# A hybrid two-layer trunk: x loaded first, one norm for all tokens, and the first projections with the features as the outer loop

## The chip, the cores and the metric

The kernel runs on one core of a Trainium2 chip. The metric is the device time of one execution in microseconds (us), as the median of repeated runs. TensorE (PE in the rows) does the matrix products, VectorE (DVE), ScalarE (ACT) and GpSimd (POOL) the elementwise work, and transfers are issued from the queues of SyncE (SP) and ScalarE.

## The reference, cut to what matters

A step of a flow-matching model: 128 context tokens and 512 latent tokens, 1024 features, two layers. The even layer has attention (grouped queries) and a gated DeltaNet behind one combined input projection, the odd layer a Mamba-2 scan, and each layer a squared-ReLU MLP. Shift, scale and gate of every sub-layer come from SiLU(cond) by a weight matrix `w_mod`. What the change touches is the beginning of the even layer:

```python
mod = (jax.nn.silu(cond) @ w_mod[layer] + b_mod[layer])[:, None, :]
sh1, sc1, g1, sh2, sc2, g2 = jnp.split(mod, 6, axis=-1)
h = rms_norm(x, norm_mix_g) * (1 + sc1) + sh1
aq, ak, av, dqkv, dz, dbeta, dalpha = _split(h @ w_in, EVEN_SPLITS)
# attention from aq, ak, av; delta rule from dqkv, gated by dz, with
beta = sigmoid(dbeta)
log_decay = -exp(a_log) * softplus(dalpha + dt_bias)
```

`aq` has 512 columns; `ak`, `av`, `dbeta` and `dalpha` together have 272. All is float32.

## The kernel before, in words

A float32 operand is held as two halves of the format fp32r, `hi` and `lo`, and a product is three matrix products: hi·hi, hi·lo, lo·hi. A weight block is loaded as 1 MB into a tile `wraw` on SyncE's queue (`wload`, L264), cast to `whi` on ScalarE (L272), and `wlo` is the rest (L275). When `self.share` is set, L275 alternates between VectorE and GpSimd by the count `self.turn`. The normed and modulated activations stand as `hh` and `hl`, features on partitions, eight groups k of 128 features.

A list scheduler orders each engine's instructions: the program is written in one order, and a simulated timeline decides what is issued first on each engine. An engine then runs its own list strictly in that order; a waiting instruction holds up all behind it.

The start, in `even()`: xt, 2.5 MB, is loaded on ScalarE's queue (L728), beside the first `w_mod` blocks on SyncE's. `token_r` works out the norm's factor twice, for tokens 0 to 319 and 320 to 639: squares on ScalarE (L577), sums over features on TensorE (L579, L585), an inverse root on VectorE (L234 to L239), and a broadcast on TensorE (L594) with a copy (L596) as `rb`. `mod_first` makes shift and scale in four chunks c of two feature groups each, from two 1 MB blocks a chunk (L516, product `modps`). `modulate` makes `hh` and `hl` (L622 to L624), for all eight groups of the first half of the tokens, then of the second. The combined projection (L750, product `atps`) has three column blocks as its outer loop: first the 272 columns, then twice 256 of the queries; inside it the five groups of 128 tokens, and innermost k and the three products. Each group's sum has one PSUM bank and is copied to `qkv` (L752).

`gates` (L883 to L915) makes beta and the log decay from 16 of the 272 columns (`gxa`, softplus in L246 to L257, `gg`), sums the decays over the chunk on TensorE (L904, from `gg`), and transposes them there (L911, from `gc`).

What follows is called the delta stage here: `delta_in` for four heads (L300, products `gps` of 322 columns with the convolutions on VectorE, L658 to L680, of which `vt` feeds `kvps`, L870), the preparation of attention between head 0 and head 1 (`att_prep`; rms factors in L1159 to L1161, scaling in L1194 and L1195, rotation in L1203 to L1208, four pieces of it on GpSimd in L1206), and the next chunks of the modulation (`mod_steps`, loads in L466, products in L459). It ends where `X` is fetched back from `growd` (L933).

Of the kernel before, what the change touches and what calls it, by code (L numbers as in the profile page):

```python
# [11 lines left out]
F32 = mybir.dt.float32  # L12
F32R = mybir.dt.float32r
I32 = mybir.dt.int32
AF = mybir.ActivationFunctionType
ALU = mybir.AluOpType
# [24 lines left out]
AS, HB = 10, 4  # L41
# [161 lines left out]
class Prog:  # L203
# [293 lines left out]
    def mod_first(self, pools, gates):  # L497

        nc = self.nc
        n = 0  # L500
        for c in range(4):
            raws = []
            if c == 1:
                gates()
            for kh in range(2):
                raw = pools[n % len(pools)].tile([P, 2048], F32, name="wraw", tag="wraw")
                n += 1
                o = self.widx["mod0", c, kh]
                self.behind = nc.sync.dma_start(out=raw, in_=self.io["wall"][o:o + P * 2048].rearrange("(p x) -> p x", p=P))
                raws.append(raw.rearrange("p (k m c) -> p k m c", k=4, c=P))  # L510
            if c == 3:
                self.setup_rest()
            ps = self.pmod.tile([P, 512], F32, name="modps", tag="mod")
            for k in range(KT):
                for r in range(4):
                    nc.tensor.matmul(ps[32 * r:32 * r + 32, :P], self.condst[:, k, 32:64], raws[k // 4][:, k % 4, :, 32 * r:32 * r + 32],  # L516
                                     start=k == 0, stop=k == KT - 1)
            t = self.small.tile([P, P], F32, name="modt", tag="modt")
            nc.vector.transpose(out=t, in_=ps[:, :P])
            cut = lambda ap: ap.rearrange("p (q m) o -> p q m o", q=2)[:, :, 2 * c:2 * c + 2]  # L520
            b = self.par(("bmod", 0))[:, 0:16].rearrange("p (m o) -> p m o", o=1)
            nc.vector.tensor_tensor(out=cut(self.mod[0][:, 0:16, :]), in0=t.rearrange("p (q m c) -> p q m c", q=2, c=32)[:, :, :, 0:3:2],
                                    in1=cut(b).to_broadcast([P, 2, 2, 2]), op=ALU.add)
# [44 lines left out]
    def token_r(self, pool, tiles, n, hf):  # L568

        nc = self.nc  # L570
        nk = len(tiles)
        c = slice(hf * HU, (hf + 1) * HU)
        inv = 1.0 / n
        ps = self.pn.tile([P, 512], F32, name="stps", tag="n")
        for k, x in enumerate(tiles):
            sq = pool.tile([P, HU], F32, name="sq", tag="sq", bufs=4)
            nc.scalar.activation(out=sq, in_=x[:, c], func=AF.Square)  # L577
            r = 32 * (k % 4)
            nc.tensor.matmul(ps[r:r + 32, :HU], self.ones32, sq, start=k < 4, stop=k >= nk - 4)  # L579
        st = pool.tile([P, HU], F32, name="st", tag="st")  # L580
        nc.vector.tensor_copy(st, ps[:, :HU])
        cuts = ((0, 128), (128, 256), (256, 320))
        pc = self.pn.tile([P, 512], F32, name="stc", tag="n")
        for t, (a, b) in enumerate(cuts):
            nc.tensor.matmul(pc[:b - a, t:t + 1], st[:, a:b], self.cst("stat"), start=True, stop=True)  # L585
        ms = pool.tile([P, 3], F32, name="ms", tag="ms", bufs=2)
        r = pool.tile([P, 3], F32, name="rr", tag="rr", bufs=2)
        nc.vector.memset(ms[64:, 2:3], 1.0)
        nc.vector.tensor_scalar(out=ms[:, 0:2], in0=pc[:, 0:2], scalar1=inv, scalar2=EPS, op0=ALU.mult, op1=ALU.add)
        nc.vector.tensor_scalar(out=ms[:64, 2:3], in0=pc[:64, 2:3], scalar1=inv, scalar2=EPS, op0=ALU.mult, op1=ALU.add)  # L590
        self.rsqrt(pool, r, ms, [P, 3])
        pb = self.pn.tile([P, 512], F32, name="rbps", tag="n")
        for t, (a, b) in enumerate(cuts):
            nc.tensor.matmul(pb[:, a:b], r[:b - a, t:t + 1].to_broadcast([b - a, P]), self.ident[:b - a, :b - a], start=True, stop=True)  # L594
        rb = pool.tile([P, HU], F32, name="rb", tag=f"rb{hf}")
        nc.vector.tensor_copy(rb, pb[:, :HU])  # L596
        return rb

    def modulate(self, h, pool, rbs):


        nc = self.nc
        a = pool.tile([P, KT, 2], F32, name="mA", tag="mA")
        n = KT // 4
        for c in range(0, KT, n):
            nc.vector.scalar_tensor_tensor(out=a[:, c:c + n], in0=self.modv(0, 1)[:, c:c + n], scalar=1.0,
                                           in1=self.par(("gmix", 0))[:, c:c + n].rearrange("p (m o) -> p m o", o=1).to_broadcast([P, n, 2]),
                                           op0=ALU.add, op1=ALU.mult)
        sh = self.modv(0, 0)
        hh, hl = h  # L610

        plan = (((slice(1, 129), CTX_U, 0), (slice(130, 322), slice(128, HU), 1)), ((slice(322, 642), slice(HU, NTOK), 1),))
        self.padding(pool, h)

        def half(hf):
# [1185 lines left out]
```

## Time and profile before

| | us |
|---|---|
| median of 3 runs | 2151.09 (2150.94 to 2152.92) |
| profiled execution, device time | 2148.23 |
| profiled execution, span of the trace | 2146.4 |
| TensorE busy in the span | 2054.9 (96%) |
| VectorE, ScalarE, GpSimd busy | 1373.3, 898.4, 153.4 |
| start: until the last product of the combined projection | 0 to 87.4 |
| delta stage | 88.2 to 225.1 |

The device time of the profiled execution is 1.8 us more than its span and 2.9 us less than the median of the runs. In rows of the timeline the first two columns are start and duration in us. Matrix products overlap on TensorE, so the time that one costs in a stream is the step between two starts, not its duration.

### The profile page before, as it was taken

How to read it: one execution, taken by the hardware profiler on the slowest of the kernel's cores; microseconds unless marked ns; L12 is line 12 of the kernel's file. 1: busy time of each engine (PE TensorE's matmuls, PEld its weight loads, DVE VectorE, ACT ScalarE, POOL GpSimd, SP SyncE). 2: the span in 40 equal slices, each digit the busy share in tenths (PEclk: the TensorE clock that was granted, in tenths of full speed). 3: DMA queues.
4: the chain of work that ended last, by engine and by line, in shares of the span. 5: the costliest groups of instructions: out<-in, count | busy, mean ns of one | idle time of the engine just before them, and what ended most of it. 6: DMA issues, size and time to landing. Idle time of an engine off the chain costs nothing.

```text
span 2146.4 us, 32954 instructions
## 1 busy us (share of the span) xinstructions
PE 2054.9 (96%) x13339; PEld 1846.3 (86%) x13339; DVE 1373.3 (64%) x2585; ACT 898.4 (42%) x1892; POOL 153.4 (7%) x112
## 2 busy tenths in 40 slices
PE   6999799899899999999899999999999899999998
PEld 4999787787797989898799999999888898989896
DVE  6376776865787767673678886787644734344445
ACT  4345444444342323233258876666531322323131
POOL 1041301300000000000000001111110000000000
PEclk9999799899999999999999999999999999999999
DMA  8261100005255344332224433343341221212121
GB/s 328 91 234 40 39 1 18 18 1 201 80 194 193 138 140 155 138 119 103 89 83 162 132 135 120 120 138 123 107 168 69 89 97 61 79 59 99 59 79 50
DMA packets 56106, 233.32 MB, mean 109 GB/s; under 512 B 6602, under 2 KB 21458, under 8 KB 34194
## 3 DMA queue, kind: packets, MB, share of 16 engines
q1 hardware_dynamic: 45952, 216.63, 28.6%
q10 hardware_dynamic: 10002, 14.58, 1.9%
q8 instruction: 105, 1.72, 0.3%
q14 instruction: 47, 0.39, 0.1%
HBM read 222.76 MB, written 8.43 MB: 108 GB/s over the span
## 4 chain that ended last, share of the span: by engine, by line
PE 89%; DVE 7%; DMA 3%; ACT 1%; issue 1%; DVEq 0%; SPq 0%; ACTq 0%
PE gps L300 41%; PE rps L328 28%; PE atps L750 2%; PE yps L1704 2%; PE avps L1331 2%; DMA wraw<-wall 1%; PE offps L1718 1%; PE dps L1038 1%; PE stps L1735 1%; PE scps L1273 1%; DMA X<-growd 1%; PE dps L1032 1%; PE xkps L1554 1%; PE modps L459 1%; PE scps L1303 1%
## 5 line engine op out<-in xcount | busy, mean ns | idle before, releaser
L300 PE MATMUL gps<-hh,whi 128*128 128x322 f32 (+3 forms) x1552 | 488.4, 316 | 1.4 <-ACT hh L412 1.4
L300 PE MATMUL gps<-hh,wlo 128*128 128x322 f32 (+3 forms) x1552 | 486.4, 314 | 0.0
L300 PE MATMUL gps<-hl,whi 128*128 128x322 f32 (+3 forms) x1552 | 485.3, 313 | 0.0
L300 PEld LDWEIGHTS gps<-hh,whi 128*128 128x128 f32 (+1 forms) x1552 | 292.3, 189 | 7.9 <-issue 4.4
L300 PEld LDWEIGHTS gps<-hl,whi 128*128 128x128 f32 (+1 forms) x1552 | 292.4, 188 | 3.2 <-issue 2.8
L300 PEld LDWEIGHTS gps<-hh,wlo 128*128 128x128 f32 (+1 forms) x1552 | 292.4, 188 | 2.1 <-issue 1.6
L328 PE MATMUL rps<-wlo,hidh 128*128 128x512 f32 x640 | 253.3, 396 | 0.0
L328 PE MATMUL rps<-whi,hidh 128*128 128x512 f32 x640 | 252.3, 396 | 0.0
L328 PE MATMUL rps<-whi,hidl 128*128 128x512 f32 x640 | 250.5, 395 | 0.0
L272 ACT CAST whi<-wraw 128x1024 fp32r<-128x1024 f32 (+2 forms) x132 | 140.0, 1062 | 252.3 <-PE rps L328 176.3
L284 DVE TENSOR_TENSOR wlo<-wraw,whi 128x1024 fp32r<-128x1024 f32 x88 | 107.5, 1224 | 187.4 <-ACT whi L283 187.3
L300 PE MATMUL gps<-yh,whi 128*128 128x320 f32 x1024 | 227.1, 311 | 0.2 <-ACT yh L412 0.2
L275 DVE TENSOR_TENSOR wlo<-wraw,whi 128x1024 fp32r<-128x1024 f32 (+3 forms) x123 | 157.9, 1285 | 101.6 <-ACT whi L272 101.1
L283 ACT CAST whi<-wraw 128x1024 fp32r<-128x1024 f32 x88 | 91.8, 1048 | 266.2 <-PE rps L328 183.3
L300 PEld LDWEIGHTS gps<-yh,whi 128*128 128x128 f32 x1024 | 172.5, 189 | 1.0 <-ACT yh L412 0.7
L300 PE MATMUL gps<-yh,wlo 128*128 128x320 f32 x512 | 158.6, 310 | 0.0
L328 PEld LDWEIGHTS rps<-whi,hidh 128*128 128x128 f32 x640 | 120.3, 188 | 29.4 <-issue 1.2
L328 PEld LDWEIGHTS rps<-wlo,hidh 128*128 128x128 f32 x640 | 120.3, 188 | 28.8 <-issue 0.6
L328 PEld LDWEIGHTS rps<-whi,hidl 128*128 128x128 f32 x640 | 120.3, 188 | 28.6
L485 DVE SCALAR_TENSOR_TENSOR macc<-wraw,condst,macc 128x512 f32<-128x512 f32 x196 | 136.6, 746 | 6.0 <-ACT macc L488 5.9
L650 DVE TENSOR_SCALAR hr<-gps 128x320 f32<-128x320 f32 x128 | 62.6, 489 | 105.8 <-PE gps L300 105.5
L651 ACT ACTIVATE hr<-hr 128x320 f32<-128x320 f32 x128 | 60.1, 470 | 151.8 <-DVE hr L650 150.3
(428 smaller groups left out, 3560.9 us busy)
## 6 DMA issues: line engine op xcount, KB each, us to landing
wraw<-wall SPq DMA_DIRECT2D x158, 1024.0 KB
bc<-afs SPq DMA_DIRECT2D x40, 512.0 KB
Q<-afr SPq DMA_DIRECT2D x64, 128.0 KB
xt<-xt ACTq DMA_DIRECT2D x1, 2560.0 KB
X<-growd SPq DMA_DIRECT2D x8, 320.0 KB
x<-x ACTq DMA_DIRECT2D x1, 2560.0 KB
xd<-x ACTq DMA_DIRECT2D x1, 2560.0 KB
x<-xd SPq DMA_DIRECT2D x1, 2560.0 KB
```

What stands on the lines that cost most here:

```text
L272: self.nc.scalar.copy(out=hi, in_=raw[:, :, c:c + m])
L275: eng.tensor_tensor(out=lo, in0=raw[:, :, c:c + m], in1=hi.bitcast(F32), op=ALU.subtract)
L283: self.nc.scalar.copy(out=hi, in_=x)
L284: self.nc.vector.tensor_tensor(out=lo, in0=x, in1=hi.bitcast(F32), op=ALU.subtract)
L300: self.nc.tensor.matmul(ps, ws[k // KT][q // 2][:, k % KT, :], xs[q % 2][k][:, c], start=k == 0 and q == 0, stop=k == n - 1 and q == 2)
L328: nc.tensor.matmul(ps, parts[x][k][:, c], w[y][:, j, :], start=k == 0 and q == 0, stop=k == n - 1 and q == 2)
L485: nc.vector.scalar_tensor_tensor(out=a, in0=x, scalar=w, in1=a, op0=ALU.mult, op1=ALU.add)
L650: nc.vector.tensor_scalar(out=r, in0=ps, scalar1=0.0, scalar2=None, op0=ALU.max)
L651: nc.scalar.activation(out=r, in_=r, func=AF.Square)
L750: nc.tensor.matmul(ps[:, :n], x[k][:, TOFF[t]:TOFF[t] + P], w[:, k, :], start=k == 0 and q == 0, stop=k == KT - 1 and q == 2)
L1331: nc.tensor.matmul(acc, val(c, i), p, start=c == 1, stop=c == 6)
L1704: nc.tensor.matmul(py[q * 64:q * 64 + 64, pr * P:(pr + 1) * P], X[t](1 + d)[:, hh * 64:hh * 64 + 64], D[t][:, d, hh, :], start=d == 0, sto ...
```

## The change

Order of loading: xt comes first, in two halves on SyncE's queue; then the blocks of chunk 0 of `w_mod`, the two query blocks of the projection, the other chunks, and only then the constants and the block of 272 columns.

The norm is made once for all 640 tokens (`token_rows` for `token_r`). The loop over the chunks c holds everything: `mod_first(c)`, then `modulate(c)` for two feature groups and all tokens, then these two groups' products with all 512 query columns, in five PSUM banks that stay open over the four chunks. The 272 columns come after that, token group by token group, and then `gates`. `self.turn` and `self.share` are set behind the projection, so that the alternation of L275 between VectorE and GpSimd starts with another parity.

```diff
-                xload = nc.scalar.dma_start(out=self.xt, in_=io["xt"])
+                for a in (0, KT // 2):
+                    self.behind = nc.sync.dma_start(out=self.xt[:, a:a + KT // 2], in_=io["xt"][:, a:a + KT // 2])
...
-                rbs = [self.token_r(xp, [self.xt[:, k, :] for k in range(KT)], D, hf) for hf in range(2)]
-                blocks = ((272, 0), (256, 272), (256, 528))
-                watt = []
-                self.turn = 1
-                self.mod_first([self.raw, raw0], lambda: watt.append(self.wpart(self.wload(("att", 0), 272, wa), 0, 272, wa)))
+                raws = [self.landed(land, ("mod0", 0, kh)) for kh in range(2)]
+                rb = self.token_rows(xp)
...
-                half = self.modulate(h, xp, rbs)
-                self.share = True
-                half(0)
-                half(1)
-                for b, (n, c0) in enumerate(blocks):
-                    hi, lo = watt[0] if b == 0 else self.wpart(self.wload(("att", b), n, wa), 0, n, wa)
-                    for t in range(NT):
-                        ps = self.pg.tile([P, 512], F32, name="atps", tag="g")
-                        for k in range(KT):
-                            for q, (x, w) in enumerate(((xs[0], hi), (xs[0], lo), (xs[1], hi))):
-                                nc.tensor.matmul(ps[:, :n], x[k][:, TOFF[t]:TOFF[t] + P], w[:, k, :],
...
+                for c in range(4):
+                    self.mod_first(c, raws)
+                    if c == 0:
+                        for j in range(2):
+                            x = self.landed(land, ("att", 1 + j)).rearrange("p (k c) -> p k c", c=256)
...
+                    if c < 3:
+                        raws = [self.landed(land, ("mod0", c + 1, kh)) for kh in range(2)]
+                    else:
+                        self.setup_rest()
+                    self.modulate(c, h, xp, rb)
+                    for k in (2 * c, 2 * c + 1):
+                        for t in range(NT):
+                            for q, (x, w) in enumerate(triples(wq)):
+                                nc.tensor.matmul(acc[t], x[k][:, TOFF[t]:TOFF[t] + P], w[:, k, :], start=k == 0 and q == 0, stop=k == KT - 1 and q == 2)
+                wk = self.wpart(self.wload(("att", 0), 272, wa), 0, 272, wa)
+                for t in range(NT):
+                    nc.scalar.copy(out=qkv[:, t, 272:784], in_=acc[t])
+                for t in range(NT):
+                    ps = self.pg.tile([P, 512], F32, name="atps", tag="g")[:, :272]
+                    for k in range(KT):
+                        for q, (x, w) in enumerate(triples(wk)):
+                            nc.tensor.matmul(ps, x[k][:, TOFF[t]:TOFF[t] + P], w[:, k, :], start=k == 0 and q == 0, stop=k == KT - 1 and q == 2)
+                    nc.scalar.copy(out=qkv[:, t, 0:272], in_=ps)
+                self.turn, self.share = 1, True
                 self.behind = None
                 self.gates(xp, self.pmod, qkv, gt)
```

Three places of the order. On TensorE, the end of the combined projection before (`atps` of the last query columns, then the sums of the gates from `gg`, then the delta stage):

```order
L750 MATMUL atps<-wlo,hh 128x256
L750 MATMUL atps<-whi,hl 128x256
L904 MATMUL gps<-gg,con 128x20 [waits DMAHW5_49,DVE_49,PE_49]
L904 MATMUL gps<-gg,con 128x20 x3
L300 MATMUL gps<-hh,whi 128x322
L300 MATMUL gps<-hl,whi 128x322
```

The same place now, where the last `atps` is of the 272 columns:

```order
L749 MATMUL atps<-wlo,hh 128x272
L749 MATMUL atps<-whi,hl 128x272
L903 MATMUL gps<-gg,con 128x20 [waits DMAHW7_49,DVE_49,PE_49]
L903 MATMUL gps<-gg,con 128x20 x3
L910 MATMUL gps<-con,gc 40x128 [waits DVE_49,Activation_49]
L300 MATMUL gps<-hh,whi 128x322
```

The sums of the gates now stand behind the very columns that they are made from, and the transpose of `gc` (L910, L911 before) has come ahead of the first L300. On VectorE, the gates before, behind the last `hl` of the modulation:

```order
L624 SCALAR_TENSOR_TENSOR hl<-htmp,mod_71,hh 128x320 [waits Activation_49] x2
L894 TENSOR_TENSOR gxa<-qkv,prm 128x40 [waits Activation_49]
L246 SCALAR_TENSOR_TENSOR spe<-gxa 128x40 [waits DVE_49]
L275 TENSOR_TENSOR wlo<-wraw,whi 128x2048 [waits DMAHW7_49,PE_49,Activation_49]
L892 TENSOR_SCALAR beta<-gx 128x20 [waits Activation_49]
```

And now, where `kst` and `asel` are small preparations of attention:

```order
L609 SCALAR_TENSOR_TENSOR hl<-htmp,mod_71,hh 128x512 [waits Activation_49]
L1215 CAST kst_1386<-ones_72 64x1792 [waits PE_49]
L1217 TENSOR_TENSOR asel<-con 4x2 [waits DMAHW3_49]
L893 TENSOR_TENSOR gxa<-qkv,prm 128x40 [waits Activation_49]
L891 TENSOR_SCALAR beta<-gx 128x20 [waits Activation_49]
```

The cast of `kst`, which stood behind the gates before, now stands ahead of them and itself waits for TensorE. On GpSimd, the begin of the delta stage before:

```order
L1168 MEMSET vc 128x640 [waits PE_49,Pool_49]
L275 TENSOR_TENSOR wlo<-wraw,whi 128x1024 [waits PE_49,DMAHW1_49,Activation_49,Pool_49]
L275 TENSOR_TENSOR wlo<-wraw,whi 128x1024 [waits DMAHW3_49,PE_49,Activation_49]
L1206 TENSOR_TENSOR ar<-qkv,con 128x10x16 [waits DMAHW5_49,DVE_49]
L1206 TENSOR_TENSOR ar<-qkv,con 128x10x16 x3
```

And now:

```order
L1167 MEMSET vc 128x640 [waits DVE_49,PE_49]
L1205 TENSOR_TENSOR ar<-qkv,con 128x10x16 [waits DMAHW2_49,DMAHW7_49,DVE_49,Activation_49]
L1205 TENSOR_TENSOR ar<-qkv,con 128x10x16 x3
L275 TENSOR_TENSOR wlo<-wraw,whi 128x1024 [waits PE_49,DMAHW2_49,Activation_49,Pool_49]
L1205 TENSOR_TENSOR ar<-qkv,con 128x10x16 [waits DVE_49]
```

The low half of head 0's second weight block (L275) now stands on GpSimd behind the first four pieces of the rotation, where two such pieces stood ahead of all rotations.

## Rows read from the trace of the kernel before

**Rows 1.** The page: its chain of waits by engine

```profile
PE 89%; DVE 7%; DMA 3%; ACT 1%; issue 1%; DVEq 0%; SPq 0%; ACTq 0%
```

**Rows 2.** Windows: us, busy by engine, clock, DMA share, GB/s

```profile
0.00:14.00 14.00, 1.94 (x32) 1.39 (x32) 1.47 (x11) 1.50 (x2) 0.20 (x4) 1.00 0.86 349
14.00:25.00 11.00, 7.67 (x118) 4.71 (x118) 4.68 (x14) 6.44 (x13) 0.00 (x0) 1.00 1.01 419
88.20:225.10 136.90, 135.68 (x1220) 130.66 (x1220) 96.33 (x195) 65.29 (x181) 35.59 (x28) 1.00 0.34 119
```

**Rows 3.** TensorE's waits: engine, line, releaser, total us, times, longest

```profile
PE atps L750 <- DVE hl L624: 3.6, 1, 3.6
...
PE kvps L870 <- DVE vt L679: 0.7, 1, 0.7
```

**Rows 4.** Timeline of ScalarE: squares behind xt, cast of a query block

```profile
14.94 1.55 ACT L577 ACTIVATE sq<-xt 128x320 f32<-128x320 f32 x4 [8.37 <-DMA xt<-xt]
...
40.05 1.89 ACT L272 CAST whi<-wraw 128x2048 fp32r<-128x2048 f32 x1
```

**Rows 5.** Timeline of VectorE: the modulation at 41, the low half at 62

```profile
41.17 6.21 DVE L622 SCALAR_TENSOR_TENSOR htmp<-xt,mA,rb 128x320 f32<-128x320 f32 x4
...
61.99 2.29 DVE L275 TENSOR_TENSOR wlo<-wraw,whi 128x2048 fp32r<-128x2048 f32 x1 [1.37 <-ACT whi L272]
```

**Rows 6.** Timeline of GpSimd: the start and the first rotations

```profile
42.02 4.54 POOL L275 TENSOR_TENSOR wlo<-wraw,whi 128x2048 fp32r<-128x2048 f32 x1 [41.58 <-ACT whi L272]
...
113.09 2.61 POOL L275 TENSOR_TENSOR wlo<-wraw,whi 128x1024 fp32r<-128x1024 f32 x1 [15.47 <-ACT whi L272]
117.93 4.06 POOL L1206 TENSOR_TENSOR ar<-qkv,con 128x160 f32<-128x160 f32 x4 [2.24 <-DVE qkv L1195]
```

**Rows 7.** Chain of waits: start us, us, what

```profile
60.65 1.32 PE gps L300 x9
61.98 25.38 PE atps L750 x216
```

**Rows 8.** Timeline of TensorE: one chunk's half; 512 columns; the gates' sums

```profile
21.39 1.08 PE L516 MATMUL modps<-wraw,condst 128*32 128x128 f32 x32
...
87.20 0.96 PE L904 MATMUL gps<-gg,con 128*128 128x20 f32 x8
...
654.81 0.40 PE L328 MATMUL rps<-whi,hidh 128*128 128x512 f32 x1
...
657.14 0.40 PE L328 MATMUL rps<-wlo,hidh 128*128 128x512 f32 x1
```

**Rows 9.** Window behind the wait that ended at 47.9

```profile
48.00:52.00 4.00, 4.00 (x20) 0.57 0.00 0
```

**Rows 10.** Timeline of VectorE: the gates, and attention's first cast

```profile
60.18 0.20 DVE L894 TENSOR_TENSOR gxa<-qkv,prm 128x40 f32<-128x40 f32 x1 [3.91 <-ACT qkv L752]
...
64.20 0.25 DVE L892 TENSOR_SCALAR beta<-gx 128x20 f32<-128x20 f32 x2
64.36 0.18 DVE L248 TENSOR_SCALAR spz<-spe 128x40 f32<-128x40 f32 x1
...
67.80 0.20 DVE L899 SCALAR_TENSOR_TENSOR gg<-gg,gea 128x40 f32<-128x40 f32 x1
...
87.34 1.09 DVE L1216 CAST kst<-ones 64x1792 fp32r<-64x1792 f32 x1 [19.35 <-PE atps L750]
```

**Rows 11.** The delta stage: VectorE's scaling (timeline), then the chain

```profile
110.42 5.97 DVE L1194 TENSOR_TENSOR qkv<-qkv,ars 128x640 f32<-128x640 f32 x5
...
127.39 1.07 DVE vt L679
...
225.07 6.63 DMA X<-growd
```

More of the change, by code (lines that the diff above doesn't have):

```diff
@@ L495, in mod_steps @@
             yield
-    def mod_first(self, pools, gates):
-        nc = self.nc
[L500 to L513, printed above, removed]
-            for k in range(KT):
[L515 to L523, printed above, removed]
@@ L565, in setup_rest, with token_rows @@
         nc.vector.tensor_scalar(out=self.prm[:, a:b], in0=self.prm[:, a:b], scalar1=0.5, scalar2=None, op0=ALU.mult)
-    def token_r(self, pool, tiles, n, hf):
+    def token_rows(self, pool):
         nc = self.nc
[L571 to L582, printed above, removed]
-        pc = self.pn.tile([P, 512], F32, name="stc", tag="n")
[L584 to L596, printed above, removed]
-        return rb
@@ L599, in modulate @@
[L599 to L608, printed above, removed]
+        pl, pc = (self.pn.tile([P, 512], F32, name="stps", tag="n") for _ in range(2))
@@ new lines, in token_rows @@
+        for k in range(KT):
+            sq = pool.tile([P, NTOK], F32, name="sq", tag="sq", bufs=2)
+            nc.scalar.activation(out=sq, in_=self.xt[:, k], func=AF.Square)
+            r = slice(32 * (k % 4), 32 * (k % 4) + 32)
+            nc.tensor.matmul(pl[r], self.ones32, sq[:, LAT_U], start=k < 4, stop=k >= KT - 4)
+            nc.tensor.matmul(pc[r, :P], self.ones32, sq[:, CTX_U], start=k < 4, stop=k >= KT - 4)
+        st = pool.tile([P, NTOK], F32, name="st", tag="sq", bufs=2)
+        nc.vector.tensor_copy(st[:, CTX_U], pc[:, :P])
@@ new lines, in token_rows @@
+        nc.scalar.copy(out=st[:, LAT_U], in_=pl)
+        pc = self.pn.tile([P, 512], F32, name="stc", tag="n")
+        for t in range(NT):
+            nc.tensor.matmul(pc[:, t:t + 1], st[:, t * P:(t + 1) * P], self.cst("stat"), start=True, stop=True)
+        ms, r = (pool.tile([P, NT], F32, name=n, tag=n) for n in ("ms", "rr"))
+        nc.vector.tensor_scalar(out=ms, in0=pc[:, :NT], scalar1=1.0 / D, scalar2=EPS, op0=ALU.mult, op1=ALU.add)
+        self.rsqrt(pool, r, ms, [P, NT])
+        rb = pool.tile([P, NTOK], F32, name="rb", tag="rb")
@@ new lines, in token_rows, with modulate @@
+        for a, b in ((0, 1), (1, NT)):
+            pb = self.pn.tile([P, 512], F32, name="rbps", tag="n")
+            for t in range(a, b):
+                nc.tensor.matmul(pb[:, (t - a) * P:(t - a + 1) * P], r[:, t:t + 1].to_broadcast([P, P]), self.ident, start=True, stop=True)
+            (nc.scalar.copy if a else nc.vector.tensor_copy)(out=rb[:, a * P:b * P], in_=pb[:, :(b - a) * P])
+        return rb
+    def modulate(self, c, h, pool, rb):
+        nc, v = self.nc, self.nc.vector
+        ks = slice(2 * c, 2 * c + 2)
+        a = pool.tile([P, 2, 2], F32, name="mA", tag="mA", bufs=2)
+        v.scalar_tensor_tensor(out=a, in0=self.modv(0, 1)[:, ks], scalar=1.0,
+                               in1=self.par(("gmix", 0))[:, ks].rearrange("p (m o) -> p m o", o=1).to_broadcast([P, 2, 2]),
+                               op0=ALU.add, op1=ALU.mult)
@@ L626, in modulate @@
-        return half
+        for j in range(2):
+            k = 2 * c + j
+            t = pool.tile([P, NTOK], F32, name="htmp", tag="htmp", bufs=2)
+            for dst, src, q in ((CTX_P, CTX_U, 0), (LAT_P, LAT_U, 1)):
+                v.scalar_tensor_tensor(out=t[:, src], in0=self.xt[:, k, src], scalar=a[:, j, q:q + 1], in1=rb[:, src], op0=ALU.mult, op1=ALU.mult)
+                nc.scalar.activation(out=hh[:, k, dst], in_=t[:, src], func=AF.Identity, bias=sh[:, k, q:q + 1])
+                v.scalar_tensor_tensor(out=hl[:, k, dst], in0=t[:, src], scalar=sh[:, k, q:q + 1], in1=hh[:, k, dst].bitcast(F32), op0=ALU.add, op1=ALU.subtract)
@@ L725, in even @@
                 xp, raw0, wa, self.pn, self.pmod, self.pg = self.pools(
[L726 removed]
+                    e2, ("ex", 1, "right"), ("raw0", 2, "left"), ("w_att", 1, "left"), ("pn0", 2, None), ("pmod0", 1, None), ("pg0", 5, None))
                 self.xt = xp.tile([P, KT, NTOK], F32, name="xt")
[L728 to L731 removed]
@@ L740, in even @@
[L740 to L752 removed]
+                triples = lambda w: ((xs[0], w[0]), (xs[0], w[1]), (xs[1], w[0]))
```

52 lines of the change are left out of this document (32 added, 20 removed).

## The prediction

> **What bounds the kernel now.** I read the page's chain first: TensorE holds 89% of it [rows 1]. Over the whole kernel, then, only TensorE's gaps and its clock can be won or lost, and the change touches nothing behind the start but the order that it leaves to the scheduler. The windows come next. The stretch from 0 to 14 us has TensorE busy for 1.94 us while DMA moves 349 GB/s, the next 11 us have 7.67 busy at 419 GB/s: a stage that loads. From 88.2 to 225.1 us TensorE is busy for 135.68 of 136.90 us [rows 2]: a stage bound by TensorE, with 1.2 us of gaps. TensorE's waits name what is late between the two: 3.6 us for `hl` (VectorE), and later 0.7 us for `vt` [rows 3]. The chain shows the projection's last stretch as an unbroken stream, 216 products of 256 columns in 25.38 us, 0.1175 us each, after nine products of the delta stage that were done early, 1.32 us [rows 7]. So the new start can gain what TensorE idles there, and the sum has to follow the chain up to the first L300, and then ask whether the delta stage keeps the gain.
>
> **When the first query product starts.** Now xt (2.62 MB), chunk 0 and both query blocks (four of 1.05 MB) and 0.1 MB of constants come first, 6.9 MB. At 349 GB/s 4.9 MB are in by 14.0 us; the other 2.0 MB at 419 GB/s take 4.9 us: 18.9 us [rows 2]. One more us from the last byte to the reader is my choice; no row bounds it better than 0 to 2. The squares no longer wait for the whole of xt until 14.94 [rows 4]. The cast of the second query block takes 1.89 us [rows 4] and ends at 21.8. On VectorE its low half and that of the block before, 2.29 us each [rows 5], are ordered in front of the copy of `rb`; the first is behind the inverse root and ends at about 22.8, the second at 25.1. With the copy, one scaling and one `hh` (about 1 us together) the first product starts at 26.1 us.
>
> **The query products.** 120 products of 512 columns. Such a product steps by 0.233 us elsewhere (ten steps from 654.81 to 657.14) [rows 8], so 28.0 us; 240 of 256 columns at 0.1175 are 28.2 [rows 7], so the wider form saves nothing. Between them stand five halves of the later chunks at 1.08 us [rows 8], 5.4 us; the modulation of the last chunk, some seven small VectorE and ScalarE steps, is not covered, 2.0 us. Those of chunks 1 and 2 are covered by chunk 2's products and by queued `atps`; without that cover they cost 1.5 to 2 us each. The clock: behind the wait that ends at 47.9 it is 0.57 over 4 us [rows 9], that is the lower of its two levels (1.2 and 2.4 GHz) for some 3.4 us, and costs 1.7 us. TensorE again idles ahead of the first product, so 1.7 us once. Sum: 26.1 + 28.0 + 5.4 + 2.0 + 1.7 = 63.2 us.
>
> **What goes.** The stall of 3.6 us [rows 3] came from four scalings that took 6.21 us [rows 5] beside GpSimd's 4.54 us for a low half [rows 6]. No such block lies on GpSimd now while the queries run, except one of 1024 columns near 50 us.
>
> The Trainium skill, page "SBUF — State Buffer", section "Who interferes with whom", says that a VectorE instruction with two SBUF inputs and a GpSimd instruction that reads SBUF exclude each other, and that the one issued second waits. Rows 5 and 6 agree. By that rule a GpSimd block that moves takes its stall along: some 2 us, an estimate from the shorter block's row.
>
> **The 272 columns.** 120 products, by columns 272/256 of 0.1175 [rows 7], 0.125 each: 15.0 us, to 78.2 us. Before, the last product of the projection ended at 87.4. The head start is 9 us there.
>
> **The gates.** Before, `gxa` ran at 60.18 and the log decay `gg` was ready at 68.00 [rows 10], under 25 us of query products, and L904 never waited. Now the columns that it needs are the last, and TensorE's next instruction waits for it, with all L300 behind. The chain: copy of the last token group, under the cast of `kst` that stands ahead on VectorE (1.09 and 0.15); `gxa` 0.2, beta 0.4, `spe` and an exponential on ScalarE 0.7; from `spz` to the end of `gg` 3.64 (64.36 to 68.00) [rows 10]. With the hops 6.2 us, to 84.4. Then the sums of L903, 0.96 [rows 8], a copy and the transpose, 0.6: the first L300 at 86.0. Bounds: 3.64 + 1.6 if everything ahead were hidden, 9 if casts or copies fall in between. I take 6.2, since all its pieces have rows.
>
> Before, L300 went on at 87.20 + 0.96 = 88.16 [rows 8], with 1.32 us of it done [rows 7]: like a start at 86.8. So 0.8 us is left of the 9.
>
> **The delta stage.** Its products need 135.7 + 1.3 = 137.0 us [rows 2, 7]. TensorE idles some 7 us ahead of it, longer than the wait ahead of rows 9, so the low clock costs 1.7 more. And VectorE comes from further back: before, its work on attention had 9 us of products to begin under; now head 0's convolutions are ordered behind the scaling of attention (5.97 us for five) [rows 11], and `vt`, done at 128.46 or 40.3 us after L300's start with 0.7 us of waiting [rows 3, 11], comes at about 42 us by the order, while TensorE is there at 39.6 (40.3 less its wait): 2.4 us. On GpSimd the low half of a weight block (2.61 us) now stands behind four rotations (4.06) [rows 6]; its tile is loaded anew by SyncE, and the next blocks of `w_mod` are queued behind that load. Below, the two are bounded by 0 (other products fill in), above by 9 (all of 2.61 + 4.06, and 2.4 for `vt`). I take 4.0, which is `vt` and a quarter of the late tile: the stage had only 1.2 us of gaps with a similar crowd on VectorE.
>
> **Sum.** 86.0 + 137.0 + 1.7 + 4.0 = 228.7 us, against 225.07, where the fetch of `X` begins [rows 11]: 3.6 us later. From the end of attention on both orders are alike, so nothing is added there; small differences before it may be worth 3 us either way. The profiled execution (2148.23) would become 2151.8; it is 2.9 below the median of the runs, and I carry the difference to that: 2151.1 + 3.6 = 2154.7 us.
>
> **Rivals.**
> - *The head start lands.* The clock doesn't fall at 26 us (TensorE has norm and chunk products there), the chain of the gates costs 5.2, and VectorE keeps up in the delta stage, as its 96 busy us of 137 [rows 2] suggest: 78.2 − 1.7 + 5.2 + 1.6 = 83.3, plus 137.0 and the 1.7 of the clock and no stall, 222.0: 3 us faster; without the second fall of the clock 4.8. Against it: the order of the DVE and POOL queues above. 2146.3 to 2148 us.
> - *The delta stage is thrown out of step.* One mechanism: the tile behind GpSimd's four rotations is late, SyncE's queue holds back the `w_mod` blocks, TensorE waits at L459, its clock falls again, and `vt` slips further as its VectorE neighbours wait for GpSimd. It decides from the point where that low half ends later than TensorE reaches the next modulation products. Price: the upper bound 9 in place of 4.0, and 1.7 of clock: 2161.4 us; with a tile that is half as late, 2158. For it: the 4.8 us that rows 5 and 6 show for one such meeting; against it: 1.2 us of gaps in that stage now [rows 2].
> - *Loading decides, nothing is gained up to 78.* If the chunks' later blocks, which wait for tiles, land late, the last chunk comes 4 to 5 us later: 2159 us.
>
> The same page of the Trainium skill, "SBUF — State Buffer", section "A bandwidth-pool intuition that's wrong (but worth ruling out)", gives about 358 GB/s between HBM and a core. The 419 GB/s of rows 2 are above that, so the measurement decides; by the page's figure the first 6.9 MB would take 19.3 us instead of 18.9 (an estimate), and the sum would be 0.4 us more.
>
> **How the numbers follow.** The forecast, head start spent on gates, clock and a slower delta stage, gets 0.55, with 2150 to 2158; the gain that lands 0.22; the stage out of step 0.13, loading 0.10. A measurement of this kernel can tell about 0.2%, 4.3 us, from no change. Of the forecast's half some 0.29 lies within that, 0.24 above and 0.02 below; of the first rival 0.13 within and 0.09 more than 4.3 us faster, since the terms there add up to a bit more if both falls of the clock go; 0.04 of loading stays within. An order whose small differences help adds 0.05 to faster, taken from within. So faster 0.16, same 0.41, slower 0.43. The range of 8 in 10 takes the first rival with half its spread and most of the second: 2145 to 2162 us.
>
> **What would show it.** In the profile after: the first 512-column product near 26 us and the last 272-column one near 78; a wait of TensorE for `gg` of 6 to 7 us in front of L903 and a window of half clock behind it; the first L300 near 86; waits at `kvps` for `vt` and at L459 for a block of 2 us each; `X` fetched near 229. The forecast is wrong if no wait stands in front of L903, if the stage from there to `X` takes 138 us or less, or if the last `atps` ends past 83.

## The result, and the profile after

The changed kernel takes 2165.81 us (median of 4 runs, 2165.10 to 2167.03), the kernel before 2151.53 (4 runs beside it, 2150.94 to 2152.92): a ratio of 1.0071, with a 95% interval from 1.0059 to 1.0084. It is slower by 14.3 us; the forecast was 3.6 us, and the time lies above the stated range. Medians here and below leave out one slow execution, of b_hold, which took 3214.03 us at a mean granted clock of 0.58.

TensorE's waits up to 250 us, columns as in [rows 3]:

```profile
PE gps L903 <- issue: 6.2, 1, 6.2
...
PE kvps L869 <- DVE vt L662: 2.9, 2, 2.6
...
PE modps L459 <- DMA wraw<-wall: 0.9, 2, 0.5
```

The wait for `hl` of 3.6 us [rows 3] is gone; the first row is the wait for the log decay in its place, 2.9 instead of 0.7 us are waited for `vt`. The chain of waits of the changed kernel (start us, us, what) from the last query products to the end of the delta stage:

```profile
59.79 5.80 PE atps L741 x25
65.59 15.08 PE atps L749 x120
80.67 6.23 issue
86.90 1.88 PE gps L903 x8
...
89.39 0.40 PE gps L910
89.79 6.90 PE gps L300 x38
...
111.42 3.11 POOL ar L1205 x3
114.54 2.36 POOL wlo L275
...
117.82 8.92 DMA wraw<-wall
...
132.74 0.84 DVE vt L662
```

The projection ends at 80.67 (87.36 before [rows 7]), but L300 starts at 89.79 (88.16 before, with nine products done [rows 7, 8]). Then the late low half on GpSimd stands in the chain, the block that waits behind it on SyncE's queue, and at last `vt`. VectorE in the same place (timeline):

```profile
80.70 1.60 DVE L1215 CAST kst<-ones 64x1792 fp32r<-64x1792 f32 x1 [19.90 <-PE atps L749]
...
82.39 0.20 DVE L893 TENSOR_TENSOR gxa<-qkv,prm 128x40 f32<-128x40 f32 x1
...
86.60 0.20 DVE L898 SCALAR_TENSOR_TENSOR gg<-gg,gea 128x40 f32<-128x40 f32 x1
```

It had been idle for 19.9 us, and begins the gates that ran at 60 to 68 us before [rows 10] only when the last product is out. Windows of the changed kernel (columns as in [rows 2]): the wait and the sums, the begin of the delta stage, the whole of it, and the stretch from the fetch of `X` at 233.67 to the norm behind the output projection (the eight `hps` products of L409 that start at 595.08, called the mark below):

```profile
80.70:89.80 9.10, 2.28 (x10) 2.19 (x11) 5.79 (x24) 1.24 (x6) 0.63 (x1) 0.77 0.07 15
89.80:93.30 3.50, 3.50 (x17) 3.50 (x17) 1.00 (x2) 1.74 (x3) 0.00 (x0) 0.62 0.15 43
89.80:233.70 143.90, 140.10 (x1228) 134.45 (x1228) 95.80 (x191) 65.39 (x179) 40.48 (x28) 0.98 0.31 112
233.70:595.10 361.40, 324.96 (x1976) 269.58 (x1974) 241.39 (x620) 153.93 (x380) 47.36 (x36) 0.89 0.16 51
```

The delta stage has 3.8 us of gaps (1.2 before [rows 2]) and a mean clock of 0.98, 143.9 us in all against 136.9. A second profile of the kernel before (b_again below) has, for its delta stage and for the stretch from X to the mark:

```profile
88.40:225.20 136.80, 135.56 (x1219) 130.56 (x1219) 96.32 (x195) 65.25 (x180) 35.61 (x28) 1.00 0.33 119
225.20:582.60 357.40, 321.21 (x1975) 266.47 (x1973) 244.23 (x620) 153.14 (x380) 47.64 (x36) 0.91 0.16 52
```

The two ends of the last stretch in the chains of waits, the changed kernel's X and mark, then the mark of the kernel before in its first profile:

```profile
233.67 6.89 DMA X<-growd
...
595.08 1.94 PE hps L409 x8
```

```profile
578.98 1.94 PE hps L409 x8
```

So the profiles place the loss, against the second profile of the kernel before: 8.4 us up to X (233.67 against 225.22), 4.0 from there to the mark (361.4 against 357.4, at a clock of 0.89 against 0.91 and with the same gaps, 36 us), 1.6 behind it: 14.1 in all, close to the medians' 14.3. Against the first profile it is 8.6, 7.5 and 1.4, 17.5 in all.

### The profile page after: what moved, and what is told of

Its sections match the earlier page's. It is cut to its first block, busy times and chain, and to the rows that moved or that the text cites. A ratio compares the mean times of both kernels' runs of the same rounds, so it can differ in the third digit from the quotient of the medians.

```text
span 2164.0 us, 32676 instructions
## 1 busy us (share of the span) xinstructions
PE 2067.2 (96%) x13215; PEld 1848.0 (85%) x13215; DVE 1362.8 (63%) x2552; ACT 900.0 (42%) x1873; POOL 153.0 (7%) x111
## 4 chain that ended last, share of the span: by engine, by line
PE 88%; DVE 5%; DMA 3%; ACT 2%; issue 1%; POOL 0%; SPq 0%; DVEq 0%; ACTq 0%; POOLq 0%
PE gps L300 41%; PE rps L328 28%; PE yps L1703 2%; PE avps L1330 2%; PE atps L741 1%; DMA wraw<-wall 1%; PE offps L1717 1%; PE stps L1734 1%; PE scps L1272 1%; DMA X<-growd 1%; PE dps L1031 1%; PE dps L1037 1%; PE modps L459 1%; PE atps L749 1%; PE xkps L1553 1%
## 5 line engine op out<-in xcount | busy, mean ns | idle before, releaser
L300 PE MATMUL gps<-hh,whi 128*128 128x322 f32 (+3 forms) x1552 | 490.4, 317 | 1.4 <-ACT hh L412 1.4
L300 PE MATMUL gps<-hh,wlo 128*128 128x322 f32 (+3 forms) x1552 | 487.5, 314 | 0.0
L300 PE MATMUL gps<-hl,whi 128*128 128x322 f32 (+3 forms) x1552 | 487.0, 314 | 0.0
L300 PEld LDWEIGHTS gps<-hh,whi 128*128 128x128 f32 (+1 forms) x1552 | 293.3, 189 | 8.0 <-issue 4.9
L300 PEld LDWEIGHTS gps<-hl,whi 128*128 128x128 f32 (+1 forms) x1552 | 293.7, 189 | 3.4 <-issue 3.0
L300 PEld LDWEIGHTS gps<-hh,wlo 128*128 128x128 f32 (+1 forms) x1552 | 293.5, 189 | 2.2 <-issue 1.8
L328 PE MATMUL rps<-wlo,hidh 128*128 128x512 f32 x640 | 253.3, 396 | 0.0
L328 PE MATMUL rps<-whi,hidh 128*128 128x512 f32 x640 | 252.3, 396 | 0.0
L328 PE MATMUL rps<-whi,hidl 128*128 128x512 f32 x640 | 250.5, 395 | 0.0
L272 ACT CAST whi<-wraw 128x1024 fp32r<-128x1024 f32 (+1 forms) x130 | 136.6, 1052 | 254.9 <-PE rps L328 176.3
L300 PE MATMUL gps<-yh,whi 128*128 128x320 f32 x1024 | 227.0, 311 | 0.2 <-ACT yh L412 0.2
L275 DVE TENSOR_TENSOR wlo<-wraw,whi 128x1024 fp32r<-128x1024 f32 (+1 forms) x122 | 153.8, 1262 | 104.9 <-ACT whi L272 104.5
L300 PEld LDWEIGHTS gps<-yh,whi 128*128 128x128 f32 x1024 | 172.3, 189 | 1.0 <-ACT yh L412 0.7
L300 PE MATMUL gps<-yh,wlo 128*128 128x320 f32 x512 | 158.5, 310 | 0.0
L328 PEld LDWEIGHTS rps<-whi,hidh 128*128 128x128 f32 x640 | 120.3, 188 | 29.4 <-issue 1.2
L328 PEld LDWEIGHTS rps<-wlo,hidh 128*128 128x128 f32 x640 | 120.3, 188 | 28.8 <-issue 0.6
L328 PEld LDWEIGHTS rps<-whi,hidl 128*128 128x128 f32 x640 | 120.3, 188 | 28.7
```

The source lines that it names most:

```text
L272: self.nc.scalar.copy(out=hi, in_=raw[:, :, c:c + m])
L275: eng.tensor_tensor(out=lo, in0=raw[:, :, c:c + m], in1=hi.bitcast(F32), op=ALU.subtract)
L300: self.nc.tensor.matmul(ps, ws[k // KT][q // 2][:, k % KT, :], xs[q % 2][k][:, c], start=k == 0 and q == 0, stop=k == n - 1 and q == 2)
L328: nc.tensor.matmul(ps, parts[x][k][:, c], w[y][:, j, :], start=k == 0 and q == 0, stop=k == n - 1 and q == 2)
```

## The experiments

In each profile the same three places are read: the first fetch of X, the mark, and the end. The table has the time of X and the stretch from X to the mark, the device time of the profiled execution, and the median of the runs, all in us. Behind the mark every kernel takes 1567 to 1571 us. The ratio is to the kernel before on the same chip, with its 95% interval; medians were taken on several chips, so small differences are to be read from the ratios.

| kernel | X | X to mark | profiled | median | ratio |
|---|---|---|---|---|---|
| before | 225.07 | 353.9 | 2148.23 | 2151.09 | |
| b_again | 225.22 | 357.4 | 2151.88 | (one run) | |
| changed | 233.67 | 361.4 | 2165.74 | 2165.81 | 1.0071 (1.0059 to 1.0084) |
| gates_late | 218.52 | 364.0 | 2152.45 | 2151.16 | 1.0012 (0.9993 to 1.0031) |
| flip | 236.46 | 357.8 | 2164.18 | 2166.94 | 1.0066 (1.0046 to 1.0087) |
| keys_first | 230.61 | 348.1 | 2150.08 | 2146.29 | 0.9972 (0.9963 to 0.9982) |
| gates_split | 224.46 | 347.9 | 2143.02 | 2145.94 | 0.9975 (0.9961 to 0.9988) |
| shift_late | 234.45 | 362.8 | 2166.13 | 2165.00 | 1.0067 (1.0045 to 1.0088) |
| keys_late | 224.76 | 377.7 | 2173.28 | 2172.59 | 1.0097 (1.0077 to 1.0117) |
| b_qfirst | 231.79 | 343.8 | 2146.66 | 2145.72 | 0.9970 (0.9959 to 0.9980) |
| b_hold | 235.37 | 349.0 | 2154.70 | 2156.57 | 1.0018 (0.9999 to 1.0036) |
| keys_split | 224.42 | 346.4 | 2141.37 | 2141.57 | 0.9954 (0.9939 to 0.9969) |
| after_ab0 | 234.66 | 355.2 | 2162.97 | 2162.97 | 1.0068 (1.0041 to 1.0095) |
| after_0123 | 234.80 | 352.2 | 2156.24 | 2156.34 | 1.0039 (1.0023 to 1.0055) |
| before_ab0 | 224.76 | 350.4 | 2145.59 | 2145.13 | 0.9975 (0.9960 to 0.9990) |

**The kernel before once more.** No edit. 

> The kernel before, unchanged, in a second profile. The two profiles so far differ by 17.5 us, the medians by 14.3. Theory A: the places where the change loses time are fixed by the order of the instructions, and the first profile of before is typical up to the fetch of X (225.1, within 0.5 us); the 3 us by which it lies below its median are at one later place, near the first weight block of the output projection (its products from 512.1). Theory B: executions scatter by some us all over; then the fetch of X moves by 2 us or more.

X at 225.22, within 0.2 us of the first profile. (The changed kernel is less firm: X lies at 233.67 to 234.80 in the four profiles with its order up to there.) The 3.5 us by which the two profiles differ lie between X and the mark (353.9 and 357.4) with the same instructions in the same order. Theory A, with the place wider than it said.

**Gates behind head 0's projections.**

```diff
-                self.gates(xp, self.pmod, qkv, gt)
...
                 self.delta_in(tp, pm, 0, xs, dn[0], self.mod_steps([(0, (2, 3, 4))], mraw, tp))
+                self.gates(tp, self.pmod, qkv, gt)
                 keys = self.att_prep(ap, ak, pat, qkv)
```

> The changed kernel with the call of gates moved behind head 0's projections, so that L300 stands directly behind the last 272-column product and the sums from gg come some 350 products later. Theory A (the wait for gg is a loss of its own: 6.2 us of idle TensorE, 2.9 for the sums and the transpose at half clock, 1.2 of clock behind it): the first L300 at 81 instead of 89.8, the fetch of X at 225 to 227 instead of 233.7, the time 2157 to 2159. Theory B (VectorE, which has attention's preparation and the convolutions to do after the projection, sets the pace of the delta stage): L300 at 81 as well, but the waits for vt and for the late weight tile grow by what is won; X at 231 to 233.7, the time 2163 to 2166.

The scheduler now lets 43 products of L300 run in the gaps of the query products, so the last `atps` ends at 85.55 and X comes at 218.52, 15 us earlier and earlier than either theory said. The delta stage (windows, columns as in [rows 2]) has a full clock and 1.6 us of gaps:

```profile
85.60:218.50 132.90, 131.29 (x1193) 126.25 (x1192) 97.60 (x215) 64.77 (x183) 30.45 (x24) 1.00 0.33 123
218.50:582.60 364.10, 318.79 (x1976) 264.16 (x1975) 246.30 (x620) 152.52 (x380) 52.51 (x41) 0.91 0.16 51
```

The time is 14.7 us below the changed kernel's by the medians, some 13 by the ratios. VectorE did not take the gain back, so theory B falls; but the stretch to the mark is the longer one. The edit takes away TensorE's wait and also puts VectorE's gates later, so alone it does not tell the two apart.

**The other parity of L275.**

```diff
-                self.turn, self.share = 1, True
+                self.turn, self.share = 0, True
```

> The changed kernel with the other parity of the alternation of L275 (self.turn = 0), which puts head 0's second low half on GpSimd ahead of the first four rotations instead of behind them. Theory A (the late tile holds back the w_mod block behind it on SyncE's queue, 117.8 to 126.8 in the chain): the chain no longer goes over that block, the fetch of X 2.5 to 4 us earlier, 230 to 231, the time 2162 to 2163. Theory B (vt, late on VectorE behind attention's scaling, ends the same wait anyway): X within 1 us of 233.7, the time 2165 to 2166.

No gain: from the first L903 (90.01 here, 86.90 there) to X 146.5 us against 146.8. The block is still waited for, its tile now released by TensorE's own products of the modulation (chain of waits):

```profile
119.73 1.05 PE modps L459 x32
...
120.81 9.04 DMA wraw<-wall
...
135.66 0.82 DVE vt L662
```

No gain from the earlier tile, then, as theory B had it, though X and the time lie above its figures. X itself is 2.8 us later since this execution had lost 1.5 us by its third query product (30.93 against 29.41) and 1.6 in the last chunk's. The run does not show that GpSimd's block costs nothing: the other parity puts another low half there (132.67 for 2.38 us), which again meets a VectorE instruction, now closely ahead of the last `vt` (timeline of VectorE):

```profile
132.75 2.99 DVE L1207 TENSOR_TENSOR qkv<-ay,ar 128x640 f32<-128x640 f32 x1 [0.82 <-POOL ar L1205]
```

**The 272 columns in the open banks, the queries behind.**

```diff
-                            for q, (x, w) in enumerate(triples(wq)):
-                                nc.tensor.matmul(acc[t], x[k][:, TOFF[t]:TOFF[t] + P], w[:, k, :], start=k == 0 and q == 0, stop=k == KT - 1 and q == 2)
+                            for q, (x, w) in enumerate(triples(wk)):
+                                nc.tensor.matmul(acc[t], x[k][:, TOFF[t]:TOFF[t] + P], w[:, k, :], start=k == 0 and q == 0, stop=k == KT - 1 and q == 2)
...
+                    ps = self.pg.tile([P, 512], F32, name="atps", tag="g")
...
+                            for q, (x, w) in enumerate(triples(wq)):
```

> The changed kernel with x first, one norm and the feature loop kept, but with the 272 columns in the five open banks of the loop and the 512 query columns behind it, token group by token group. gxa can start under the 28 us of query products. Theory A (what the change loses at the projection is the gates' wait, by the queries coming first): the last atps at 74 to 80, no wait ahead of L902, the first L300 at 76 to 81, X at 221 to 226, the time 2146 to 2152. Theory B (VectorE paces the delta stage): X at 229 or later, 2156 to 2162.

The time of theory A, with neither its L300 nor its X. The chain of waits at the end of the projection:

```profile
63.44 23.98 PE atps L748 x103
...
87.44 1.37 DVE kst L1214
...
88.91 0.21 DVE gc L903
...
89.49 0.29 PE gps L909
89.78 7.02 PE gps L300 x47
```

`gg` was ready, but the transpose of `gc` still held TensorE, behind the cast of `kst`; L300 starts where it does in the changed kernel. X is 3.1 us earlier, the stretch to the mark 13.3 us shorter. Most of the gain lies in a part of the program that the edit does not touch.

**Only the sums late.**

```diff
-        ps = pm.tile([P, 512], F32, name="gps", tag="mod")
+
+    def gate_sums(self, tp, pm, gt):
+
+        nc, v, g = self.nc, self.nc.vector, gt["gg"]
+        ps = pm.tile([P, 512], F32, name="gps", tag="mod")
...
                 self.delta_in(tp, pm, 0, xs, dn[0], self.mod_steps([(0, (2, 3, 4))], mraw, tp))
+                self.gate_sums(tp, self.pmod, gt)
```

> The changed kernel with the gates cut in two: VectorE's chain from gxa to gg stays where it was, directly behind the projection; only the sums and the transpose on TensorE (L903, L910) are written behind head 0's projections, so that L300 may pass them. Theory A (the loss is TensorE being held behind L903): the first L300 right behind or before the last 272-column product, X at 218 to 222 as in gates_late, the time 2149 to 2153. Theory B (VectorE's 6 us of gates ahead of attention's preparation and the convolutions are the loss, wherever TensorE waits): X at 225 or later, 2156 to 2162.

VectorE does the gates where the changed kernel does them, and TensorE passes on (chain of waits: L300 between the query products, the sums at 150.87):

```profile
69.41 1.53 PE gps L300 x10
70.94 15.06 PE atps L750 x120
...
124.57 1.03 DVE vt L662
...
150.87 0.80 PE gps L909 x8
```

X is 9.2 us earlier than in the changed kernel, the median 19.9 us lower and below the kernel before. X lies between the two theories (218 to 222, and 225 or later). Most of what gates_late won at X is TensorE let go; the last 5.9 us are not, and here TensorE waits for `vt` of VectorE longer than in any of the kernels above (TensorE's waits up to 240 us):

```profile
PE kvps L871 <- DVE vt L662: 4.3, 2, 4.0
```

Of the 22.7 us between this profile and the changed kernel's, 13.5 lie again between X and the mark.

**The loads of shift.**

```diff
+                for q, j in shift:
+                    with self.tc.issue_after(self.loads[0].ins):
+                        nc.sync.dma_start(out=shift[q, j], in_=self.modr[0][3, q:q + 1, j * 512:j * 512 + 512].to_broadcast([P, 512]))
```

> The changed kernel with the loads of shift (L806) pinned behind the first weight block of the output projection on SyncE's queue, the order that the kernel before had there. Theory A (the weight block stood behind a load that waits for VectorE, 511.83 to 512.26 in the chain, and came 3 to 4 us later against the third fetch of X than before, 124.7 us against 121.3): from the third fetch of X to the first L328 136 to 137 us instead of 140, the time 2162 to 2163. Theory B (attention's own chain ends later by as much, and the block would have waited for it anyway): the stretch stays at 139 to 141, the time 2165 to 2166.

From the third fetch of X (391.25) to the first L328 (530.70) 139.5 us, the time as before: theory B's figures. That attention's own chain sets the end there is argued from it, not traced.

**Both edits.** keys_first and gates_late together. 

> Both edits together: the 272 columns in the loop's open banks, the queries behind them, and the call of gates behind head 0's projections. Theory A (each edit takes away a wait of its own; keys_first still has 3.4 us of TensorE's gaps and 1.7 of clock in the delta stage, and 1.3 us of wait at the transpose): X at 222 to 227 instead of 231, the time 2140 to 2144. Theory B (the later stage, attention, gives back what comes early, as it did in gates_late, where 15 us at X were 11 at the output projection): 2145 to 2149.

X at 224.76, as theory A had it; then 377.7 us to the mark, and the slowest kernel of all. It is slower than the kernel before, where both theories had it faster.

**Queries first in the kernel before.**

```diff
-                blocks = ((272, 0), (256, 272), (256, 528))
+                blocks = ((256, 272, 1), (256, 528, 2), (272, 0, 0))
```

> The kernel before with one part of the change alone: the query blocks first, the 272 columns last (and the first query block loaded early in place of the 272 columns). Here the scheduler puts the sums of the gates (L904) some 66 L300 behind the last atps, so that TensorE isn't held by gg. Theory A (the loss of the change is the hold): nearly no change, the first L300 directly behind the last atps, the time 2149 to 2155. Theory B (queries first is the loss in itself, since VectorE gets the keys, the gates and attention's work only at the end of the projection): X at 230 or later, 2157 to 2165.

Both theories are half right: X at 231.79, 6.6 us later than before, as B had it; and yet 0.3% faster, since the stretch behind X takes 343.8 us. The part of the change that I held for the culprit loses up to X even where nothing is held.

**The hold alone.** The same kernel, with

```diff
+                with self.tc.issue_after(self.hold.ins) if self.hold and k == q == 0 else nullcontext():
```

on the first product of each sum of head 0 (L300), where `hold` is the last of the gates' sums. 

> The same kernel, queries first in the kernel before, with L300 of head 0 pinned behind the sums of the gates, as the scheduler had it in the changed kernel; nothing else is edited. Theory A (the hold costs its 6 us, 2 to 3 us of sums at half clock, and then gaps and clock in the delta stage and attention): 10 to 16 us slower than the same kernel without the pin, 2160 to 2168. Theory B (only the visible wait counts, and VectorE, which works in the meantime, gives part of it back): 3 to 7 us slower, 2153 to 2160.

The wait is there (chain of waits), 5.80 us and the sums at half clock:

```profile
86.15 5.80 issue
91.95 1.86 PE gps L907 x8
```

X moves by 3.6 us, the mark by 8.8 (584.41 against 575.62), the ratio from 0.9970 to 1.0018, some 10 us; its executions spread over 10 us, so the size is firm to a few us only. It lies between the two theories: behind the sums L300 goes on at 93.82, 6.2 us later than in b_qfirst; the delta stage takes 2.6 of them back and attention adds 5.2.

**Keys first, sums late.** 

> The 272 columns in the open banks, the queries behind them, and the gates cut in two as in gates_split, with the sums behind head 0's projections. Theory A (the late sums alone helped; keys_late lost in attention because VectorE's chain of the gates was late as well): at or below the two, 2140 to 2146. Theory B (any order in which the delta stage runs ahead meets the same crowd in attention): TensorE's clock and gaps between the first fetch of X and the norm behind the output projection take 360 us or more instead of 348, 2155 to 2172.

2141.57 us, 0.9954 (0.9939 to 0.9969): the fastest of all, faster than both kernels. Up to the end of the delta stage TensorE and VectorE have the same list as in keys_late (the scheduler left VectorE's gates where they were in both), and X comes at the same time (224.42 and 224.76). Windows from there to the mark, keys_late first:

```profile
224.80:602.40 377.60, 328.63 (x1975) 273.14 (x1974) 247.70 (x620) 152.69 (x380) 51.43 (x41) 0.89 0.15 49
```

```profile
224.40:570.80 346.40, 311.66 (x1975) 259.48 (x1974) 237.13 (x620) 153.25 (x380) 47.20 (x36) 0.93 0.16 54
```

The same 1975 products, 31 us apart: 49 us of gaps against 35, and a clock of 0.89 against 0.93.

One place of it can be read. GpSimd's list is not the same up to X: it makes attention's masks (`qm`, `nm`) at 159 us in keys_split, and in keys_late only at 242.47, among its pieces of the delta rule's `M`. Beside them two VectorE steps of ten columns take 2.2 us each, where the same lines take 0.17 a little earlier, and TensorE stands 15.83 us until VectorE's `M` is there (keys_late, timelines of VectorE and TensorE):

```profile
239.32 0.17 DVE L239 SCALAR_TENSOR_TENSOR drs<-rsa,drs 128x10 f32<-128x10 f32 x1
...
242.65 2.18 DVE L238 SCALAR_TENSOR_TENSOR rsa<-rsa,dss 128x10 f32<-128x10 f32 x1
244.87 2.24 DVE L239 SCALAR_TENSOR_TENSOR drs<-rsa,drs 128x10 f32<-128x10 f32 x1
```

```profile
252.13 2.05 PE L974 MATMUL dps<-dq,kT 128*128 128x128 f32 x8 [15.83 <-DVE M L953]
```

gates_late, the other kernel with the whole call of gates late, also has the masks behind X (236.06) and also waits 15.83 us for `M`; no other kernel here waits for longer than 7.5 us between X and the mark. How much of the wait the masks cause was not tested; VectorE's own order ahead of `M` may be part of it.

**Only attention's interleaving.** In `even()`, the string that says in which order attention's steps (letters) and the four delta heads (digits) are written:

```diff
-            for ch in "0abcdefghi123":
+            for ch in "ab0cdefghi123":
```

and, for after_0123, "0123abcdefghi". 

> The changed kernel with two groups of attention's steps written ahead of the first delta head. The order of all engines is the same up to TensorE's row 1336, behind the first fetch of X; from there attention and the delta rule are interleaved in another way. Theory A (attention's interleaving, which the scheduler makes anew whenever something ahead of it moves, is worth several us by itself): the first fetch of X at 233 to 236 as before, and the stretch from there to the norm behind the output projection away by 4 us or more from the 358 to 363 of the changed kernel's runs, to either side. Theory B (that stretch is set by what reaches it late, not by its order): 358 to 363.

 

> The changed kernel with all four delta heads written ahead of attention's steps; the order is the same up to TensorE's row 1175, again behind the first fetch of X. Theory A: the first fetch of X at 233 to 236, the stretch behind it away by 4 us or more from 358 to 363. Theory B: 358 to 363.

 

> The kernel before with two groups of attention's steps written ahead of the first delta head; the order is the same up to TensorE's row 1461. Theory A: the first fetch of X at 225 to 226, the stretch behind it away by 4 us or more from the 354 to 357 of the kernel before. Theory B: 354 to 358.

X stays within 1.2 us of the unedited kernel in each (234.66, 234.80; 224.76). Behind it: after_ab0 355.2, 2.6 us below the lowest of the three runs that have the changed kernel's order there (flip; in shift_late all but the last part), after_0123 352.2, 5.6 below it; before_ab0 350.4, 3.5 below the lower of two. Against the highest it is 7.6, 10.6 and 7.0. after_0123 is some 7 us faster than the changed kernel by the ratios (1.0039 against 1.0071; 9.5 by the medians), before_ab0 0.25% faster than before; after_ab0, at 1.0068, is no faster than the changed kernel. Theory A for after_0123; the other two go its way in the stretch, but miss its 4 us against the nearest run. Row of after_0123 (windows):

```profile
234.80:587.00 352.20, 317.30 (x1975) 260.21 (x1974) 240.81 (x620) 152.05 (x380) 46.92 (x36) 0.93 0.16 53
```

## Why the prediction was wrong

*What was right.* The first loads and squares; 15.0 us for the 272 columns (15.08); the chain of the gates, 6.2 us (6.23), with TensorE's whole list behind it; the delta stage with its gaps, 142.7 us (143.9): TensorE idles there for 3.8 us where 4.0 were forecast, and is busy for 140.1 where 138.7 were, since the clock costs more than the 1.7 put down (a mean of 0.98 over the stage, that is about 2.9 us). The head start of the projection was spent, as forecast.

VectorE was held by GpSimd's moved block as forecast (timeline of VectorE, changed kernel; the block runs from 114.54 for 2.36 us, and the same instruction takes 0.83 at 129.85, with no such block beside it):

```profile
114.57 3.00 DVE L1207 TENSOR_TENSOR qkv<-ay,ar 128x640 f32<-128x640 f32 x1 [0.38 <-POOL ar L1205]
```

The Trainium skill's rule, page "SBUF — State Buffer", section "Who interferes with whom", that the second of the two waits, agrees with that row, 2.2 us. What the stall costs is open: flip moves the block, but has a stall of the same size.

*The start of the delta stage, mis-sized by 3.8 us.* The first query product came at 27.70 instead of 26.1: TensorE had idled for 4.5 us for `rr` and made the broadcast and the next chunk's products at half clock (timelines of TensorE and VectorE, changed kernel):

```profile
23.45 2.50 PE L588 MATMUL rbps<-con,rr 128*128 128x128 f32 x10 [4.55 <-DVE rr L239]
25.88 1.88 PE L513 MATMUL modps<-wraw,condst 128*32 128x128 f32 x32
```

```profile
21.03 2.29 DVE L732 TENSOR_TENSOR wql<-wraw,wqh 128x2048 fp32r<-128x2048 f32 x1
23.23 0.16 DVE L239 SCALAR_TENSOR_TENSOR rr<-rsa,rr 128x5 f32<-128x5 f32 x1
```

I had the first low half of the query blocks (L732) behind the inverse root; it stands ahead of the root's last step (L239), and TensorE waits for both. From there to the end of the query products it was 37.9 us for the 37.1 of the forecast. I had put the clock's 1.7 us once into the query products; the low clock came ahead of them (0.51 from 23.4 to 27.7), and the products and the chunks' halves took as much more instead. Together: 80.67 instead of 78.2. And L903 to L910 took 2.9 us instead of 1.6, as the sums run at half clock right behind the wait (1.88 against 0.96 [rows 8]).

*The step that failed: "From the end of attention on both orders are alike, so nothing is added there; small differences before it may be worth 3 us either way".* The forecast for the profiled execution was 2151.8, and it took 2165.74: 5.0 us of the 13.9 lie at X (233.67 instead of 228.7) and 8.9 behind it, where nothing was added. Of the 8.9, 3.5 are how far the two executions of the kernel before differ, 4.0 lie in attention beyond that, 1.4 behind the mark. That stretch is not a constant to which a late start is added: with the same products it took 343.8 to 377.7 us in the kernels above. keys_late and keys_split, alike up to X on TensorE and VectorE, show that the order alone, GpSimd's and that of all engines behind X, can move it by 31 us. after_0123 shows it for the changed kernel's own code: its stretch is 5.6 us below the lowest and 10.6 below the highest of the three profiles with the changed kernel's order, and its time some 7 us below. The prediction knew of small differences there and allowed them 3 us, with no row for that figure.

*What the runs don't settle.* How much of the changed kernel's 4.0 us behind X is order and how much is scatter: two executions of one program differ there by 3.5 us. Nor what in an order makes it slow, other than the wait of 15.8 us in keys_late and gates_late, which the changed kernel does not have; for the rest the rows show only where it goes, into gaps and a clock between 0.89 and 0.93.

*Cause.* The hold is one, by one edit each way: gates_split takes it from the changed kernel (9.2 us up to X), b_hold puts it into the old one with the queries first (3.6 us up to X, 8.8 at the mark). It is not the only one: b_qfirst is 6.6 us late at X without it. Of these, 1.3 are the nine products of the delta stage that no longer run early, 3.1 are further gaps and 1.7 is clock; that VectorE's late start on attention's work makes the gaps is argued, not shown (the releasers of the two longest, 2.0 and 1.8 us, are ScalarE's `kst` and `dq`). And the gains of keys_first, gates_split and b_qfirst against the kernel before lie wholly or nearly so behind X, in an interleaving that none of them aimed at.

## What to carry to other kernels

When a scheduler orders the program anew, compare two profiles at fixed places, and ask of each stretch between them whether its own list has changed; a stage of short dependent steps can give or take more than the edit itself, so write it in two or three orders and time them. An instruction that waits on an in-order engine is priced by all that stands behind it: let it be written later, so that ready work can pass it, rather than make its wait shorter; then look again at what else the scheduler moved. And a wait is to be priced with the low clock of the instructions that follow it, from their first one on.

## What the runs showed of the hardware

TensorE's clock in a stage that does not fill it: from X to the mark it is busy for 87 to 91% of the time, and the mean granted clock is 0.89 to 0.93 in the kernels' windows; (1 − clock) times the stretch is 23 to 43 us, the gaps are 31 to 49, and both move with the order. Eight products of 20 columns took 0.80 us in gates_split, where TensorE came from other products, and 1.88 behind the wait of the changed kernel.

VectorE beside GpSimd: L1207 took 3.00 us beside GpSimd's subtraction (L275, 2.36 us) and 0.83 elsewhere, and steps of ten columns took 2.18 and 2.24 us beside GpSimd's masks (`qm`, two in 4.62 us) and 0.17 elsewhere.
